# A two-layer diffusion backbone: value products of two heads side by side, modulation sums moved behind the softmax, and the feed-forward's second half reordered

## The chip, the cores and the metric

The kernel runs on one core of one Trainium2 chip. The metric is the device time of the whole program in microseconds; the smaller the better. The number of before is the median of three runs.

## What is computed

256 latent tokens and 256 context tokens, 1024 channels wide, pass through two layers in fp32. Each layer takes a modulated norm, three token mixers (a short convolution, a gated MLP along the tokens, attention with 8 heads of 64 channels and two key/value heads), a merge by gates, and a channel mixer. Layer 0 has a dense feed-forward of width 2816, layer 1 a mixture of eight experts of which each token takes two. The modulation vectors are products of one conditioning vector with a large matrix. Cut to what the change touches:

```python
m = silu(cvec) @ w_mod[i] + b_mod[i]            # shift, scale, gate, six of each layer
h = rms_norm(x, g) * (1 + scale) + shift
s = q @ k.T * HEAD_DIM ** -0.5                  # 256 latent + 256 context keys for latent tokens
p = exp(s - max) / (sum + exp(sink - max))
o = p @ v                                       # the value products
mix = sigmoid(z_gate) * (y_branch @ w_branch)   # summed over three branches, then @ w_out
y = (silu(h @ w_gate) * (h @ w_up)) @ w_down    # the feed-forward of layer 0
```

## The kernel before

The order of the work is written out by hand, and each engine takes its instructions in the order of the program. Weights come through `Stream`: a chunk is loaded from memory (L79, SyncE's queue), ScalarE rounds it to a high part (L102), and GpSimd, in layer 1 together with VectorE, subtracts to make the low part (L106). Two pairs of buffers, `w0` and `w1`, hold such chunks in layer 0. `st.take()` hands out a chunk and queues the conversion of the next one, so in ScalarE's queue the rounding of a coming chunk stands behind whatever was queued there for the chunk before. A product of fp32 accuracy is three matmuls: high by high, high by low, low by high (`prod`, L446, L447, L449).

In `mixer`, the gate products run in three passes of eight steps (`gate_pass`, argument `kb`). A step multiplies the gate weights (24 matmuls), takes tanh on ScalarE (L714), multiplies the branch weights and adds into `mix` on VectorE (L720, or L722 and L723). Between the steps `tick` runs one `slot` of the attention. Layer 0 has 16 units in the order latent head t, latent head 4+t, context head t, context head 4+t; a latent unit has four blocks of keys, a context unit two. Layer 1 has 8 latent units. Slot j does the value product of unit j-2 (`att_d`: matmuls L624 into the one PSUM buffer `pv`, a copy on ScalarE L626, a subtraction on VectorE L627), the transposes of unit j-1 (`att_c`: L603, evicted by ScalarE L607 and for four blocks also by VectorE L609), the scores of unit j (L560, L561), the query split of unit j+1 (L542, L543), and the softmax of unit j (`att_b`: row maxima on VectorE L571 or L579, exponentials on ScalarE, then L588, L589 and the scaling L591 on VectorE).

VectorE also computes the modulation vectors of later stages in the background. `bg(n)` runs n of 128 pieces; a piece is two multiply-and-sum instructions over 512 columns (L226, in `columns`), whose elementwise result goes to a scratch tile from the rotating pool `scr` (10 buffers) and is never read. The matrix rows come over SyncE's queue into the two halves of one tile `mraw` (`mod_load`, L218), each load queued one piece ahead. The pieces 0 to 95 use a load of 512 KB twice, the pieces 96 to 127 once. In layer 0's mixer a gate step runs one piece after its tanh and one after its sum, before `tick`.

The feed-forward of layer 0 runs in two halves (`hf`). Each has 11 chunks `f` of gate and up products (22 by 24 matmuls in all), whose result is split into `ah` (ScalarE, L834) and `al` (VectorE, L835), and then 8 down products `d` that add over the 11 chunks. The steps of a chunk on VectorE are: one piece, L829, L830, one piece, L835, one piece. Then layer 1's norm, its mixer, and the experts follow.

The first down product of a half starts with the chunks in order and needs `ah[10]`, made last, in its 21st matmul:

```python
for k in ks:                       # prod, ks = range(11)
    mm(p, wh(k), ah(k)); mm(p, wh(k), al(k))
for k in ks:
    mm(p, wl(k), ah(k))
```

Of the kernel before, what the change touches and what calls it, by code (L numbers as in the profile page):

```python
# [20 lines left out]
NT = 512  # L21
# [115 lines left out]
def backbone_kernel(ctx, tc, xT, small, const, moe_const, gmw, gmb, modk, modd, wa, wg2, wg4, wo, fgu, fd, mgu, mdn, fing, out):  # L137
# [83 lines left out]
    def columns(w, l, i, vs, bias=0.0):  # L221

        for v in vs:
            for h in range(2):
                o = (modv if h else mcol)[:, l, v, i:i + 1]
                nc.vector.tensor_tensor_reduce(scr(), w[:, h * 512:(h + 1) * 512], crows[:, v, h * 512:(h + 1) * 512],  # L226
                                               scale=1.0, scalar=mcol[:, l, v, i:i + 1] if h else bias,
                                               op0=OP.mult, op1=OP.add, accum_out=o)
# [52 lines left out]
    crows = crow_stack.enter_context(tc.tile_pool(name="crows", bufs=1, side="right")).tile([128, 2, D], F32, name="crows")  # L281

    def scr(dt=F32):
        return front.tile([128, 512], dt, name="scr", bufs=10)

# [178 lines left out]
    def mixer(l, kv, extra=()):  # L464
# [20 lines left out]
        def tick(cnt=1):  # L485
            for _ in range(cnt):
                if fill:
                    fill.pop(0)()

        def block(c, col, width, nn, acts=None):  # L490
# [42 lines left out]
        units = [(s, hd) for t in range(4) for s in range(ns) for hd in (t, 4 + t)]  # L533
        U = {}

        def att_q(j):
# [74 lines left out]

        def att_d(j):
            s, hd = units[j]
            t, kv = hd % 4, hd // 4
            u = U.pop(j)
            a = slice(kv * 64, kv * 64 + 64)
            nk = 4 if s == 0 else 2
            k0 = 0 if s == 0 else 2
            if t not in yh:
                yh[t] = mp.tile([128, n], F32R, name="q", bufs=5)  # L620
                yl[t] = mp.tile([128, n], F32R, name="yl", bufs=4)
            po = psum("pv")
            for kk in range(nk):
                mm(po[a, :NX], vt[:, k0 + kk, kv * 64:kv * 64 + 64], u["pT"][kk // 2][:, (kk % 2) * NX:(kk % 2 + 1) * NX],  # L624
                   start=kk == 0, stop=kk == nk - 1)
            nc.scalar.copy(yh[t][a, s * NX:(s + 1) * NX], po[a, :NX])  # L626
            nc.vector.tensor_tensor(yl[t][a, s * NX:(s + 1) * NX], po[a, :NX], yh[t][a, s * NX:(s + 1) * NX].bitcast(F32), op=OP.subtract)  # L627

        def slot(j):
            if 0 <= j - 2:  # L630
                att_d(j - 2)
            if 0 <= j - 1 < len(units):
                if extra:
                    extra.pop(0)()
                att_c(j - 1)
            if j < len(units):
                att_a(j)
                if j + 1 < len(units):
                    att_q(j + 1)
                att_b(j)  # L640
# [5 lines left out]
        for g in range(ns):  # L646
# [8 lines left out]
            if g == 0:  # L655
                rope(q[3], q[3])
                att_q(0)
                fill += [lambda j=j: slot(j) for j in range(len(units) + 2)]
            vv = gelu2(pg, NT)
# [45 lines left out]
        def gate_pass(kb, ah, al, first, ticks):  # L705
            for d in range(KD):
# [4 lines left out]
                fh, fl = H_(n)  # L711
                prod(pg, lambda k: hg[:, k, :], lambda k: lg[:, k, :], fh, fl, range(KD), n)
                tg = scr()
                nc.scalar.activation(tg[:, :n], pg[:, :n], AF.Tanh, scale=0.5)  # L714
# [6 lines left out]
                else:  # L721
                    nc.vector.scalar_tensor_tensor(tg[:, :n], tg[:, :n], 1.0, pb[:, :n], op0=OP.add, op1=OP.mult)  # L722
                    nc.vector.tensor_tensor(mix[:, d, :], mix[:, d, :], tg[:, :n], op=OP.add)  # L723
                    if kb == 4 and d == KD - 2:
                        split_mix(0)
                        split_mix(1)
                if d < KD - 2 or kb < 4:
                    bg(rate)
                tick(ticks)

# [28 lines left out]
        while fill:  # L759
            tick()  # L760
        gate_pass(4, lambda k: yh[k][:, :], lambda k: yl[k][:, :], False, 0)

# [48 lines left out]
    for hf in range(2):  # L811
        ah, al = {}, {}
        for f in range(11):
# [9 lines left out]
            else:  # L823
                for i, p in enumerate((pg, pu)):
                    prod(p, lambda k: h[:, k, i * 128:i * 128 + 128], lambda k: g[:, k, i * 128:i * 128 + 128], fh, fl, range(KD), NT)
            bg(1)
            t = scr()
            nc.scalar.activation(t, pg, AF.Tanh, scale=0.5)
            nc.vector.scalar_tensor_tensor(t, t, 1.0, pg, op0=OP.add, op1=OP.mult)  # L829
            nc.vector.tensor_tensor(t, t, pu, op=OP.mult)  # L830
            bg(1)
            ah[f] = fp.tile([128, NT], F32R, name="ah", bufs=12)
            al[f] = fp.tile([128, NT], F32R, name="al", bufs=12)
            nc.scalar.copy(ah[f], t)  # L834
            nc.vector.tensor_tensor(al[f], t, ah[f].bitcast(F32), op=OP.subtract)  # L835
            bg(1)
        if hf == 0:
# [3 lines left out]
        for d in range(8):  # L841
            c = st.take()
            h, g = (a[:, :1408].rearrange("p (k c) -> p k c", k=11) for a in (c.hi, c.lo))
            p = psum("mm")
            prod(p, lambda k: h[:, k, :], lambda k: g[:, k, :], lambda k: ah[k][:, :], lambda k: al[k][:, :], range(11), NT)
            for s in range(2):
                xs = x[:, d, s * NX:(s + 1) * NX]
                nc.vector.scalar_tensor_tensor(xs, p[:, s * NX:(s + 1) * NX], mcolumn(0, s, 5, d), xs, op0=OP.mult, op1=OP.add)
            if hf == 1:
                square(d, NT)  # L850
            if hf == 0 or d < 5:
                bg(1)
    ffn_stack.close()
# [693 lines left out]
```

## Time and profile before

| | us |
|---|---|
| median of three runs | 2093.8 (2092.99 to 2103.32) |
| the profiled execution, whole | 2096.31 |
| its span | 2094.2 |
| TensorE busy | 1922.0, 92% of the span |
| VectorE busy | 1300.0, 62% |
| ScalarE busy | 695.6 |
| GpSimd busy | 445.9 |

Times in rows count from the start of the span. Layer 0's mixer with attention lies between about 131 and 345 us, the feed-forward's second half between 632 and 837 us, layer 1's mixer between 850 and 1067 us, and the experts from there to the end. A row of a timeline gives the start, the duration (both in us), the engine, the line, the operation, the tiles written and read, the shape and a count; in brackets stands how long the engine sat idle before it and what ended that. `PE` is TensorE, `DVE` VectorE, `ACT` ScalarE, `POOL` GpSimd, `SPq` SyncE's DMA queue. [...]

### The profile page before, as it was taken

The page shows a single profiled execution, that of the slowest core. Times are in us where ns is not written, and L with a number is a line of the kernel's source. Part 1 is how long each engine was busy: PE and PEld are TensorE (multiplying, and loading weights), DVE is VectorE, ACT ScalarE, POOL GpSimd, SP SyncE. Part 2 cuts the span into 40 slices and gives each one's busy share as a digit, 9 for nine tenths or more (in the row PEclk, how much of TensorE's full clock was granted, in tenths as well). Part 3 has the DMA queues.
Part 4 walks back from the last instruction along what each step waited for, and adds up shares of the span by engine and source line. Part 5 has one row for each costly group of instructions (what it writes and reads, how often), then busy time and mean ns, then how long its engine had stood idle before and what let it go on. Part 6 is the DMA issues. An engine that isn't in the chain of part 4 may idle for free. (4 is left out here: it accounts for less than half of the span.)

```text
span 2094.2 us, 31796 instructions
## 1 busy us (share of the span) xinstructions
PE 1922.0 (92%) x9396; PEld 1304.7 (62%) x9396; DVE 1300.0 (62%) x1946; ACT 695.6 (33%) x903; POOL 445.9 (21%) x188
## 2 busy tenths in 40 slices
PE   7999889989999889899989999998999998898676
PEld 4777668878888668788987765644444444332122
DVE  7488789759967772766568866654454545442222
ACT  4334332332212212554546654433232322210000
POOL 4432234233443325524420000000000000000000
PEclk9999999999999989899999999999999999999888
DMA  6323134424444553433638989999899998899995
GB/s 265 117 67 122 51 126 161 156 90 171 154 148 173 178 192 130 154 104 106 232 123 284 323 304 365 343 376 416 323 370 354 360 365 337 332 389 408 403 387 206
DMA packets 79401, 506.04 MB, mean 242 GB/s; under 512 B 8784, under 2 KB 9424, under 8 KB 28880
## 3 DMA queue, kind: packets, MB, share of 16 engines
q1 hardware_dynamic: 79056, 501.64, 64.1%
q8 instruction: 193, 3.16, 0.6%
q14 instruction: 152, 1.25, 0.2%
HBM read 500.55 MB, written 1.05 MB: 240 GB/s over the span
## 5 line engine op out<-in xcount | busy, mean ns | idle before, releaser
L106 POOL TENSOR_TENSOR w0l<-raw,w0h 128x2048 fp32r<-128x2048 f32 (+6 forms) x43 | 156.0, 3628 | 242.2 <-ACT w0h L102 222.6
L106 POOL TENSOR_TENSOR w1l<-raw,w1h 128x2048 fp32r<-128x2048 f32 (+6 forms) x42 | 153.2, 3649 | 229.4 <-ACT w1h L102 215.5
L1221 PE MATMUL PO<-raw,Xo 128*64 128x512 f32 x768 | 186.3, 620 | 11.3 <-issue 10.0
L226 DVE CUSTOM_DVE_ANT_0 scr<-mraw,crows 128x512 f32<-128x512 f32 x128 | 165.3, 1292 | 40.7 <-DMA mraw<-in_modd_dram 40.6
L1061 POOL TENSOR_SCALAR P<-P,gates 128x256 f32<-128x256 f32 x16 | 22.1, 1392 | 758.4 <-PE PO L1048 622.0
L226 DVE CUSTOM_DVE_ANT_0 scr<-mraw,crows,mcol 128x512 f32<-128x512 f32 x128 | 161.1, 1259 | 4.6
L102 ACT CAST w1h<-raw 128x2048 fp32r<-128x2048 f32 (+3 forms) x82 | 142.2, 1735 | 43.4 <-PE mm L447 22.6
L102 ACT CAST w0h<-raw 128x2048 fp32r<-128x2048 f32 (+3 forms) x82 | 141.2, 1721 | 41.9 <-PE mm L447 28.8
L446 PE MATMUL mm<-Hh,w0h 128*128 128x512 f32 (+1 forms) x380 | 139.1, 376 | 10.7 <-ACT Hh L384 4.2
L446 PE MATMUL mm<-Hh,w1h 128*128 128x512 f32 (+1 forms) x384 | 137.1, 368 | 8.9 <-ACT w1h L102 7.1
L447 PE MATMUL mm<-Hl,w0h 128*128 128x512 f32 (+1 forms) x380 | 137.7, 372 | 6.2 <-POOL Hl L440 6.2
L447 PE MATMUL mm<-Hl,w1h 128*128 128x512 f32 (+1 forms) x384 | 135.6, 364 | 0.0
L1221 PEld LDWEIGHTS PO<-raw,Xo 128*64 128x64 f32 x768 | 55.3, 142 | 115.7 <-issue 114.3
L106 DVE TENSOR_TENSOR w1l<-raw,w1h 128x2048 fp32r<-128x2048 f32 (+3 forms) x49 | 103.5, 2112 | 30.9 <-ACT w1h L102 30.3
L1294 PE MATMUL PYO<-raw,ho 128*64 128x512 f32 x392 | 95.5, 620 | 11.4 <-issue 5.6
L106 DVE TENSOR_TENSOR w0l<-raw,w0h 128x2048 fp32r<-128x2048 f32 (+3 forms) x48 | 97.8, 2037 | 9.7 <-ACT w0h L102 9.0
L106 DVE TENSOR_TENSOR w2l<-raw,w2h 128x2048 fp32r<-128x2048 f32 (+3 forms) x45 | 90.9, 2020 | 19.5 <-ACT w2h L102 12.8
L1236 DVE SCALAR_TENSOR_TENSOR to<-to,PO 64x512 f32<-64x512 f32 x28 | 18.9, 676 | 126.0 <-ACTq L98 78.8
L1270 ACT COPY ho<-PO 128x256 f32<-128x256 f32 x42 | 15.7, 373 | 245.0 <-PE PO L1262 198.8
L449 PE MATMUL mm<-Hh,w0l 128*128 128x512 f32 (+1 forms) x380 | 94.3, 370 | 1.9 <-POOL w0l L106 1.9
L102 ACT CAST w2h<-raw 128x2048 fp32r<-128x2048 f32 (+2 forms) x45 | 81.5, 1811 | 35.6 <-PE PU L1214 26.0
L446 PEld LDWEIGHTS mm<-Hh,w0h 128*128 128x128 f32 x380 | 73.1, 192 | 25.2 <-ACT Hh L384 4.8
(469 smaller groups left out, 4253.9 us busy)
## 6 DMA issues: line engine op xcount, KB each, us to landing
raw<-in_mgu_dram SPq DMA_DIRECT2D x191, 1024.0 KB, 7.9
raw<-in_mdn_dram SPq DMA_DIRECT2D x97, 1024.0 KB, 8.5
mraw<-in_modd_dram SPq DMA_DIRECT2D x80, 512.0 KB, 4.8
mraw<-in_mgu_dram SPq DMA_DIRECT2D x33, 1024.0 KB, 8.1
raw<-in_fgu_dram SPq DMA_DIRECT2D x22, 1024.0 KB, 4.9
raw<-in_wg_dram SPq DMA_DIRECT2D x28, 640.0 KB, 3.9
raw<-in_wa_dram SPq DMA_DIRECT2D x15, 1024.0 KB, 5.0
mraw<-in_mdn_dram SPq DMA_DIRECT2D x15, 1024.0 KB, 7.4
```

The lines of the kernel that those rows point to most:

```text
L102: self.nc.scalar.copy(c.hi[:, :n], c.raw[:, :n])
L106: eng.tensor_tensor(c.lo[:, a:b], c.raw[:, a:b], c.hi[:, a:b].bitcast(F32), op=OP.subtract)
L226: nc.vector.tensor_tensor_reduce(scr(), w[:, h * 512:(h + 1) * 512], crows[:, v, h * 512:(h + 1) * 512], scale=1.0, scalar=mcol[:, l, v, i ...
L446: mm(p[:, :n], wh(k), ah(k), start=first and k == ks[0], stop=False)
L447: mm(p[:, :n], wh(k), al(k), start=False, stop=False)
L449: mm(p[:, :n], wl(k), ah(k), start=False, stop=last and k == ks[-1])
L1061: nc.gpsimd.tensor_scalar(P[:, i, :], P[:, i, :], gates[:, i, e:e + 1], None, op0=OP.mult)
L1221: mm(po[64 * g:64 * g + 64], xo[:, kk, :], w[:, k, g, :], start=kk == 0, stop=kk == KD - 1)
L1236: nc.vector.scalar_tensor_tensor(t, t, 1.0, g, op0=OP.add, op1=OP.mult)
L1270: modes(e, split, lambda: nc.scalar.copy(ho, po[:, 0:256]))
L1294: mm(PYO[64 * b:64 * b + 64], ho[:, ff, :], w[:, f, b, :], start=first and ff == 0, stop=last and ff == 3)
```

## The change

The elementwise result of a modulation piece goes into one fixed tile `junk`, and `scr` gets 14 buffers. The value products of two units, head t and head 4+t of the same tokens, become one step `att_d(m)`: their matmuls alternate between the columns 0 to 63 and 64 to 127 of the array, and one copy and one subtraction over 128 partitions take the place of two each over 64. The step isn't part of a slot any more; it is queued in `ready` once both units are transposed, and runs in `between()`, which a gate step calls behind its gate product and `tick` calls first. In a gate step, the second modulation piece comes behind `tick`. In the feed-forward's second half the last two chunks run no pieces; two more pieces run in the first half's down products, and every down product of the second half runs one. Every down product takes the chunks 0 to 9 first, with their low parts, and chunk 10 at the end. The memory set aside for DMA descriptors is cut to 2048 bytes, which makes room for the larger `scr`.

```diff
 def columns(...):
-                nc.vector.tensor_tensor_reduce(scr(), w[:, ...], crows[:, ...],
+                nc.vector.tensor_tensor_reduce(junk, w[:, ...], crows[:, ...],
...
+    junk = front.tile([128, 512], F32, name="junk")
-        return front.tile([128, 512], dt, name="scr", bufs=10)
+        return front.tile([128, 512], dt, name="scr", bufs=14)
...
         def tick(cnt=1):
             for _ in range(cnt):
+                between()
                 if fill:
                     fill.pop(0)()
+        def between():
+            while ready:
+                att_d(ready.pop(0))
...
-        def att_d(j):
+        def att_d(m):
...
+            pT = [U.pop(2 * m + kv)["pT"] for kv in range(2)]
             for kk in range(nk):
-                mm(po[a, :NX], vt[:, k0 + kk, kv * 64:kv * 64 + 64], u["pT"][...], start=kk == 0, stop=kk == nk - 1)
-            nc.scalar.copy(yh[t][a, s * NX:(s + 1) * NX], po[a, :NX])
-            nc.vector.tensor_tensor(yl[t][a, ...], po[a, :NX], yh[t][a, ...].bitcast(F32), op=OP.subtract)
+                for kv in range(2):
+                    a = slice(kv * 64, kv * 64 + 64)
+                    mm(po[a, :NX], vt[:, k0 + kk, a], pT[kv][...], start=kk == 0, stop=kk == nk - 1)
+            nc.scalar.copy(h, po[:, :NX])
+            nc.vector.tensor_tensor(l, po[:, :NX], h.bitcast(F32), op=OP.subtract)
         def slot(j):
-            if 0 <= j - 2:
-                att_d(j - 2)
             if 0 <= j - 1 < len(units):
                 ...
                 att_c(j - 1)
+                if j % 2 == 0:
+                    ready.append(j // 2 - 1)
...
 def gate_pass(...):
                 prod(pg, ...)
+                between()
                 tg = scr()
                 nc.scalar.activation(tg[:, :n], pg[:, :n], AF.Tanh, scale=0.5)
...
+                tick(ticks)
                 if d < KD - 2 or kb < 4:
                     bg(rate)
-                tick(ticks)
...
 for f in range(11):
-            bg(1)
+            rate = 1 if hf == 0 or f < 9 else 0
+            bg(rate)        # and so at the chunk's other two places
...
 for d in range(8):
-            prod(p, ..., range(11), NT)
+            for ks in (range(10), range(10, 11)):
+                prod(p, ..., ks, NT, first=ks[0] == 0, last=ks[0] > 0)
...
-            if hf == 0 or d < 5:
-                bg(1)
+            bg(2 if hf == 0 and d < 2 else 1)
...
-    nc = bacc.Bacc("TRN2", target_bir_lowering=False, num_devices=1)
+    nc = bacc.Bacc("TRN2", target_bir_lowering=False, num_devices=1, dynamic_dma_scratch_size=2048)
```

## Rows read from the trace of the kernel before

**Rows 1.** Busy time per stretch (columns: stretch, length, busy time and instruction count per engine).
```profile
133.00:231.00 98.00, 87.48 (x390) 66.25 (x388) 81.37 (x167) 37.16 (x84) 30.19 (x8) 0.97 0.30 107
260.00:314.00 54.00, 48.32 (x223) 36.57 (x222) 46.49 (x93) 19.70 (x43) 16.86 (x6) 1.00 0.35 123
750.00:800.00 50.00, 41.12 (x154) 32.41 (x153) 29.96 (x57) 10.97 (x12) 19.19 (x6) 0.86 0.51 175
```
**Rows 2.** Waits of TensorE and VectorE, layer 0's mixer (waited for: us, times, longest).
```profile
PE tp L603 <- DVE scr L591: 13.3, 10, 2.7
PE pv L624 <- DVE yl L627: 1.7, 1, 1.7
DVE tiny L588 <- ACT tiny L587: 25.0, 16, 1.8
```
**Rows 3.** Timeline of one gate step with its slot, layer 0, VectorE and GpSimd.
```profile
172.96 3.24 POOL L106 TENSOR_TENSOR w1l<-raw,w1h 128x1280 fp32r<-128x1280 f32 x1 [7.21 <-ACT w1h L102]
173.42 3.33 DVE L226 CUSTOM_DVE_ANT_0 scr<-mraw,crows,mcol 128x512 f32<-128x512 f32 x1
177.28 0.68 DVE L226 CUSTOM_DVE_ANT_0 scr<-mraw,crows 128x512 f32<-128x512 f32 x1
178.68 0.41 DVE L627 TENSOR_TENSOR yl<-pv,q 64x256 fp32r<-64x256 f32 x1
179.57 0.69 DVE L571 CUSTOM_DVE_ANT_0 scr<-sc,cst 128x512 f32<-128x512 f32 x1
183.31 0.88 DVE L591 TENSOR_SCALAR scr<-scr,tiny 128x512 f32<-128x512 f32 x2
184.11 3.45 POOL L106 TENSOR_TENSOR w0l<-raw,w0h 128x1280 fp32r<-128x1280 f32 x1 [7.91 <-ACT w0h L102]
```
**Rows 4.** Timeline of TensorE, eight matmuls of one column half and of alternating halves.
```profile
925.18 1.94 PE L624 MATMUL pv<-scr,vt 128*64 128x256 f32 x8
1299.96 1.94 PE L1221 MATMUL PO<-raw,Xo 128*64 128x512 f32 x8
```
**Rows 5.** Timeline, layer 0: last transposes kept waiting, VectorE's wait for TensorE between.
```profile
230.98 1.44 PE L603 MATMUL tp<-idn,scr 128*128 128x128 f32 x8 [2.74 <-DVE scr L591]
249.27 0.69 DVE L754 TENSOR_TENSOR cc<-cc,mm 128x512 f32<-128x512 f32 x1 [0.81 <-PE mm L449]
303.81 0.72 PE L603 MATMUL tp<-idn,scr 128*128 128x128 f32 x4 [1.63 <-DVE scr L591]
```
**Rows 6.** Timeline, layer 1: scalings of two units and the transposes that follow each.
```profile
917.86 0.88 DVE L591 TENSOR_SCALAR scr<-scr,tiny 128x512 f32<-128x512 f32 x2
919.86 1.04 PE L603 MATMUL tp<-idn,scr 128*128 128x128 f32 x8
...
968.28 0.88 DVE L591 TENSOR_SCALAR scr<-scr,tiny 128x512 f32<-128x512 f32 x2
968.92 1.29 PE L603 MATMUL tp<-idn,scr 128*128 128x128 f32 x8 [1.16 <-DVE scr L591]
```
**Rows 7.** Timeline of the feed-forward's second half, its last chunks and first down products.
```profile
752.36 0.62 ACT L834 CAST ah<-scr 128x512 fp32r<-128x512 f32 x1 [12.90 <-DVE scr L830]
754.83 0.80 PE L446 MATMUL mm<-Hh,w1h 128*128 128x512 f32 x1 [3.51 <-ACT w1h L102]
760.67 0.69 DVE L226 CUSTOM_DVE_ANT_0 scr<-mraw,crows 128x512 f32<-128x512 f32 x1
767.86 1.50 DVE L226 CUSTOM_DVE_ANT_0 scr<-mraw,crows 128x512 f32<-128x512 f32 x1 [4.30 <-DMA mraw<-in_modd_dram]
768.80 0.39 PE L446 MATMUL mm<-ah,w0h 128*128 128x512 f32 x1
778.19 0.79 PE L446 MATMUL mm<-ah,w0h 128*128 128x512 f32 x1 [4.67 <-ACT ah L834]
784.96 0.40 PE L446 MATMUL mm<-ah,w1h 128*128 128x512 f32 x1
```
**Rows 8.** Timeline, after the feed-forward: VectorE's first step of the norm's inverse root.
```profile
841.77 0.16 DVE L358 TENSOR_SCALAR tiny<-pv 128x4 f32<-128x4 f32 x1 [1.30 <-PE pv L354]
```

More of the change, by code (lines that the diff above doesn't have):

```diff
@@ L225, in columns @@
                 o = (modv if h else mcol)[:, l, v, i:i + 1]
-                nc.vector.tensor_tensor_reduce(scr(), w[:, h * 512:(h + 1) * 512], crows[:, v, h * 512:(h + 1) * 512],
+                nc.vector.tensor_tensor_reduce(junk, w[:, h * 512:(h + 1) * 512], crows[:, v, h * 512:(h + 1) * 512],
                                                scale=1.0, scalar=mcol[:, l, v, i:i + 1] if h else bias,
@@ L534, in mixer @@
         U = {}
+        ready = []
         def att_q(j):
@@ L610, in att_c @@
                 u["pT"].append(pT)
-        def att_d(j):
[L613 to L616, printed above, removed]
+        def att_d(m):
+            s, hd = units[2 * m]
+            t = hd % 4
             nk = 4 if s == 0 else 2
@@ L622, in att_d @@
             po = psum("pv")
+            pT = [U.pop(2 * m + kv)["pT"] for kv in range(2)]
             for kk in range(nk):
-                mm(po[a, :NX], vt[:, k0 + kk, kv * 64:kv * 64 + 64], u["pT"][kk // 2][:, (kk % 2) * NX:(kk % 2 + 1) * NX],
-                   start=kk == 0, stop=kk == nk - 1)
-            nc.scalar.copy(yh[t][a, s * NX:(s + 1) * NX], po[a, :NX])
-            nc.vector.tensor_tensor(yl[t][a, s * NX:(s + 1) * NX], po[a, :NX], yh[t][a, s * NX:(s + 1) * NX].bitcast(F32), op=OP.subtract)
+                for kv in range(2):
+                    a = slice(kv * 64, kv * 64 + 64)
+                    mm(po[a, :NX], vt[:, k0 + kk, a], pT[kv][kk // 2][:, (kk % 2) * NX:(kk % 2 + 1) * NX], start=kk == 0, stop=kk == nk - 1)
+            h, l = (y[t][:, s * NX:(s + 1) * NX] for y in (yh, yl))
+            nc.scalar.copy(h, po[:, :NX])
+            nc.vector.tensor_tensor(l, po[:, :NX], h.bitcast(F32), op=OP.subtract)
         def slot(j):
-            if 0 <= j - 2:
-                att_d(j - 2)
             if 0 <= j - 1 < len(units):
@@ L657, in mixer @@
                 att_q(0)
-                fill += [lambda j=j: slot(j) for j in range(len(units) + 2)]
+                fill += [lambda j=j: slot(j) for j in range(len(units) + 1)]
             vv = gelu2(pg, NT)
@@ L760, in mixer @@
             tick()
+        between()
         gate_pass(4, lambda k: yh[k][:, :], lambda k: yl[k][:, :], False, 0)
@@ L830, in backbone_kernel @@
             nc.vector.tensor_tensor(t, t, pu, op=OP.mult)
-            bg(1)
+            bg(rate)
             ah[f] = fp.tile([128, NT], F32R, name="ah", bufs=12)
@@ L835, in backbone_kernel @@
             nc.vector.tensor_tensor(al[f], t, ah[f].bitcast(F32), op=OP.subtract)
-            bg(1)
+            bg(rate)
         if hf == 0:
@@ L844, in backbone_kernel @@
             p = psum("mm")
-            prod(p, lambda k: h[:, k, :], lambda k: g[:, k, :], lambda k: ah[k][:, :], lambda k: al[k][:, :], range(11), NT)
+            for ks in (range(10), range(10, 11)):
+                prod(p, lambda k: h[:, k, :], lambda k: g[:, k, :], lambda k: ah[k][:, :], lambda k: al[k][:, :], ks, NT,
+                     first=ks[0] == 0, last=ks[0] > 0)
             for s in range(2):
```

1 line of the change is left out of this document (removed).

## The prediction

> **What bounds the kernel now.** I began with busy time by stretch. TensorE is near full everywhere, but in two stretches of layer 0's mixer it is busy for 87.5 of 98 us and 48.3 of 54 [rows 1], so 16.2 us are lost there. Then the waits: the transposes stand 13.3 us for the scaling that ends the softmax, once a value product for a subtraction, 1.7 us [rows 2]. So VectorE's queue is what is late. It is busy for 81.4 of the 98 us [rows 1]; add its wait for the exponentials, 25.0 us in 16 units [rows 2], nine of which (14 us) fall in this stretch, and it has under 3 us to spare. In layer 0's attention VectorE sets the pace, and what TensorE saves there isn't saved by the program. The timeline of a step shows on what it spends itself: a modulation piece takes 1.40 us (177.28 to 178.68), but one of its two instructions takes 3.33 when GpSimd's subtraction runs beside it, 2.6 more than usual; the row maxima, fed from PSUM, take 0.69 [rows 3]. Between the two stretches VectorE waits for TensorE (0.81 at 249.27 [rows 5]), so there TensorE sets the pace. In layer 1 no pieces run; TensorE waits for the scaling at the last unit only [rows 6]. In the feed-forward's second half the chain is: VectorE waits for a load of `mraw` (4.30 at 767.86), the product of the chunk stands behind that piece, `ah` behind the product, and in ScalarE's queue the rounding of a coming weight chunk behind `ah`: `ah` of chunk 8 at 752.36, chunk 10 on TensorE at 754.83 after 3.51 idle [rows 7]. The first down product stops 4.67 us for `ah` of chunk 10 [rows 7], and the granted clock over that stretch is 0.86 [rows 1].
>
> **The change, part by part.** All sums are made against the profiled execution, 2096.3 us, which is 2.5 above the median 2093.8.
>
> *Pairs in column halves.* Eight matmuls of one half with 256 columns take 1.94 us; eight of the experts, alternating between halves with 512 columns, take 1.94 too [rows 4]. So alternating doubles the columns per time, and a pair of latent units (16 matmuls) should take 2.0 instead of 3.9; a context pair 1.1 instead of 2.1. TensorE's work falls by 4 x 1.9 + 4 x 1.0 = 11.6 us in layer 0 and 4 x 1.9 = 7.6 in layer 1. Bounds: no overlap (0) and all of it.
>
> *Layer 0, to the wait at 230.98* [rows 5]. VectorE sets the pace, so I count VectorE's instructions. Seven subtractions of 0.41 [rows 3] become three over twice the partitions, which I price the same, since they have the same 256 columns: 4 x 0.42 = 1.7 saved. Moving the second piece behind the softmax doesn't shorten the queue: each scaling comes one piece earlier, but so does the one before it. The collision stays too: GpSimd started 0.8 us after the scaling began, which is where VectorE comes to the next piece [rows 3]; after the change it is the second piece of the same step instead of the first of the next. Taking the product buffer from `scr` to `junk` removes waits of ScalarE alone, which isn't late: nothing. From 231 to 260 TensorE sets the pace, and one interval between transposes loses a latent product: at most 1.9, less what VectorE allows; I take 1.3 (bounds 0 and 1.9). From 260 on VectorE sets the pace again. The first scaling there comes a piece earlier, 1.4 once, and one subtraction fewer, 0.4. The last wait for the subtraction, 1.7 [rows 2], goes, since the last pair follows a gate product. Sum: 1.7 + 1.3 + 1.4 + 0.4 + 1.7 = **6.5** (bounds: 0, and 27.8, if VectorE no longer bound: 16.2 + 11.6).
>
> The new position adds a wait. The pair's subtraction stands in VectorE's queue ahead of the next step's first piece, the sum into `mix` and the next softmax, and TensorE reaches the products only after 24 matmuls (24 x 0.235 = 5.6 us, from rows 4), 2.0 for the pair and some 0.6 for the copy: 8.2 us behind the scores. VectorE comes there after its softmax (179.57 to 184.2, 4.6 [rows 3]) and a piece of 1.4, or 4.0 beside GpSimd: 6.0 to 8.6 us after the scores if it begins at once. It begins late, for it is behind TensorE. I take 0; it costs up to 2.2 us per pair.
>
> *Layer 1.* A waiting transpose starts 0.64 after the scaling starts (968.28 to 968.92 [rows 6]). Of eight intervals between transposes four now hold a pair (2.0 for 1.9: nothing) and four hold none. These shorten by what TensorE was behind the scaling, at most 1.9: at the first, 2.00 - 0.64 = 1.4; at the last, nothing [rows 6]; the two between give 1.6 and 0.6 by the same difference. With one subtraction less in the last, 0.4: **4.0** (bounds: 0 and 7.6).
>
> *The feed-forward's second half.* Up to chunk 8 three pieces run per chunk as before, each with its own load of 512 KB from piece 96 on. Because two more pieces run early, this begins two pieces sooner. The waits sit at the same places of each chunk, since a load is queued when the piece two before is done; I charge 0.8 us (bounds: none, and two waits of 4.3 [rows 7], 8.6). In chunks 9 and 10 VectorE is free: its last piece of chunk 8 ends at 760.67 [rows 7], so `ah` of chunk 10 is made about 2 us after its products end at 768.80, and the first down product, which began there [rows 7], needs it only after 30 matmuls, 7 us. It then takes 33 x 0.23 = 7.6 and the second begins at 776.4 instead of 784.96 [rows 7]: 8.6. The stop at 754.83 stays. The eight pieces in the down products have 7.6 us each and lie beside matmuls; if a load is late there, the sum into `x` is late, and the cover is the three PSUM buffers. Only the last one is bare: its 1.4 us come before the norm's steps, where VectorE has 1.30 idle [rows 8]; I charge 0.4 (bounds 0 and 4.0, beside GpSimd). SyncE's queue: four more loads pass ahead of layer 1's first weights, and the weight load that reuses `mraw` waits for the last piece's 1.4 us; that is within the bound of the last piece. Sum: 8.6 - 0.8 - 0.4 = **7.4** (bounds: -4 and 12, the latter with the stop at 754.83 gone).
>
> The two extra pieces in the first half lie under a TensorE that never waits there: nothing. Together 6.5 + 4.0 + 7.4 = 17.9: 2078.4 against the profiled run, **2076** as a median.
>
> **The rivals.**
> *The collision goes.* If GpSimd's subtraction falls beside instructions fed from PSUM, the 13 gate steps with a slot lose 2.6 us each of VectorE (34 us), TensorE sets the pace in layer 0 and gains 27.8 instead of 6.5: 2055. For it: only the piece is stretched, the row maxima aren't [rows 3]. Against: GpSimd follows the exponentials by one rounding, and the piece follows them by the scaling, before and after. [...] Half of it would still be 2066.
> *The load waits give the feed-forward back.* Two more single loads at 4.3 us delay `ah` of chunk 8 by 8.6: that part gives 0, total 10.5: 2083.
> *The halves don't overlap.* Pairs cost 3.9: layer 1 loses 1.9 in three of four intervals and layer 0 where TensorE sets the pace (3.7): 17.9 - 9.4 = 8.5: 2085. Rows 4 speak against it.
> *TensorE's clock eats layer 0's part.* TensorE now idles longer at each scaling; at 750 to 800 us, with 9 us idle of 50, 0.86 was granted [rows 1]. If the 152 us of layer 0's two stretches ran so, TensorE would need some 20 us more, about what it has to spare: 6.5 becomes 0, 2082.
> *Slower: VectorE stands at the pair's subtraction.* If TensorE, not VectorE, is late, every one of the 12 pairs stops VectorE, with the next softmax behind it. It takes back all at 1.5 us per pair (17.9/12) and costs over 0.5% at 2.4. If the eight of layer 0 wait a whole gate product, 8 x 5.6 = 45: 2121. Against: VectorE has no idle time there but for the exponentials.
>
> **How the numbers follow.** Forecast 0.57, spread about 2067 to 2084; collision gone 0.07; load waits 0.12; no overlap 0.07; clock 0.09; slower 0.08. The range 2062 to 2089 leaves out the slower case, most of the first rival and the tails of the others, just under 2 in 10. About 0.5%, 10.5 us, is what a measurement of this kernel can tell from no change; so faster is below 2083.3. Faster: 0.52 + 0.07 + 0.05 + 0.01 + 0.06 = 0.71. Within: 0.05 + 0.07 + 0.06 + 0.03 = 0.21. Slower: 0.08.
>
> **What would show it.** Right: value products as 12 groups of 16 or 8 matmuls with about 0.12 us each; L627 twelve times at 0.42; layer 0's transposes still waiting for L591, more in sum than 13.3 us; a piece of 3.3 us in each gate step; in the feed-forward stops near chunks 7, 8 and 10, and none at the first down product; 0.4 us before the norm. Wrong: VectorE idle at L627, no stretched pieces in layer 0, or a stop at a down product.

## The result and the profile after

The changed kernel takes 2079.06 us (median; 2075.30 to 2093.04) against 2093.39 before (2088.21 to 2103.32). The ratio is 0.9938, with a 95% interval of 0.9918 to 0.9958: faster by 14.3 us, or by 9 to 17. The forecast was 2076. The profiled execution took 2076.99 us with a span of 2075.2; that of before took 2096.31 with 2094.2. Of these two, one lies 2.1 below its median and the other 2.9 above, so the traces show 19 us where the medians show 14.

The way to read two traces of one program is to set the starts of the same events side by side. The starts below are TensorE's; the last column is what the span has gained up to there, beside the forecast's sum at that point.

| event | before | after | gained | forecast |
|---|---|---|---|---|
| layer 0, 1st transposes | 140.21 | 140.66 | -0.5 | 0 |
| layer 0, 9th transposes | 230.98 | 230.14 | 0.8 | 1.7 |
| layer 0, 13th transposes | 269.38 | 265.48 | 3.9 | 4.8 |
| layer 0, last transposes | 303.81 | 298.37 | 5.4 | 4.8 |
| first norm | 440.81 | 434.84 | 6.0 | 6.5 |
| feed-forward, second half | 631.88 | 626.45 | 5.4 | 6.5 |
| its first down product | 768.80 | 762.53 | 6.3 | 5.7 |
| its second down product | 784.96 | 770.06 | 14.9 | 14.3 |
| second norm | 839.87 | 824.94 | 14.9 | 13.9 |
| layer 1, first transposes | 911.33 | 895.35 | 16.0 | 13.9 |
| layer 1, eighth transposes | 968.92 | 950.11 | 18.8 | 17.9 |
| third norm | 1067.02 | 1050.20 | 16.8 | 17.9 |
| end of the span | 2094.2 | 2075.2 | 19.0 | 17.9 |

TensorE reaches the first transposes of layer 0 without waiting in every kernel of this document, and starts them anywhere from 139.9 to 141.7 us. That spread lies ahead of what the change does, so differences in layer 0 are also counted from there below.

The page of after shows where the engines stand. TensorE is busy for 92% of the span:

```profile
PE 1903.7 (92%) x9396; PEld 1299.3 (63%) x9396; DVE 1295.3 (62%) x1934; ACT 690.9 (33%) x891; POOL 447.8 (22%) x188
```

Next is the timeline of TensorE with the value products and the transposes: start, duration, operation and, in brackets, idle time and what ended it. The first row is a pair of latent units in layer 1, the second a context pair in layer 0; then come the transposes that answer to [rows 5] and [rows 6].

```profile
907.42 1.95 PE L634 MATMUL pv<-scr,vt 128*64 128x256 f32 x16
180.35 1.08 PE L634 MATMUL pv<-scr,vt 128*64 128x256 f32 x8
...
230.14 1.29 PE L611 MATMUL tp<-idn,scr 128*128 128x128 f32 x8 [2.09 <-DVE scr L599]
298.37 0.72 PE L611 MATMUL tp<-idn,scr 128*128 128x128 f32 x4 [1.73 <-DVE scr L599]
950.11 2.06 PE L611 MATMUL tp<-idn,scr 128*128 128x128 f32 x8 [2.59 <-DVE scr L599]
```

Sixteen matmuls of a pair take 1.95 us, what eight in one half took [rows 4]. So the change does what it says. The waits of layer 0's mixer answer to [rows 2] (waited for: us, times, longest):

```profile
PE tp L611 <- DVE scr L599: 17.0, 8, 3.7
...
DVE tiny L596 <- ACT tiny L595: 25.0, 16, 1.8
```

TensorE now stands longer at the scaling, 17.0 us instead of 13.3 (its 1.7 us at the subtraction are gone), and VectorE's wait for the exponentials hasn't moved. This is what a saving looks like on an engine that wasn't the bound: its work shrinks and its waits grow. The busy times per stretch answer to [rows 1] (length; PE, PEld, DVE, ACT and POOL busy; then TensorE's granted clock as a share of full speed, DMA share and GB/s):

```profile
133.00:231.00 98.00, 85.87 (x397) 66.40 (x396) 80.82 (x166) 35.83 (x80) 30.39 (x8) 0.93 0.30 107
260.00:314.00 54.00, 49.90 (x237) 38.42 (x236) 46.62 (x88) 19.99 (x41) 20.00 (x6) 0.97 0.33 119
750.00:800.00 50.00, 48.84 (x214) 40.03 (x215) 18.59 (x34) 12.29 (x14) 29.53 (x10) 1.00 0.40 139
```

VectorE's 80.8 of 98 us are the 81.4 of before. The third stretch is the feed-forward's: 0.86 was granted there before and 1.00 now. Half of that lies behind the stop ahead of chunk 10 (0.82 from 750.0 to 768.8 before) and half in the first down product, whose stop is gone (0.79 from there to 784.96). A gate step of layer 0 answers to [rows 3]: GpSimd's subtraction and the two instructions of a piece beside it.

```profile
171.91 0.69 DVE L226 CUSTOM_DVE_ANT_0 junk<-mraw,crows 128x512 f32<-128x512 f32 x1
172.18 3.20 POOL L106 TENSOR_TENSOR w1l<-raw,w1h 128x1280 fp32r<-128x1280 f32 x1 [7.06 <-ACT w1h L102]
172.64 3.29 DVE L226 CUSTOM_DVE_ANT_0 junk<-mraw,crows,mcol 128x512 f32<-128x512 f32 x1
```

The collision has stayed. Up to layer 0's last transposes 12 piece instructions are stretched in either kernel, by 32.3 us in all before and 32.5 after (over the usual 0.72). The feed-forward's second half answers to [rows 7] and [rows 8]: the matmul of chunk 10 that had to wait, the roundings to `ah` of chunks 8 and 10, the starts of the first two down products, the last piece's instruction and the norm's first step.

```profile
749.98 0.50 PE L448 MATMUL mm<-Hh,w1h 128*128 128x512 f32 x1 [2.61 <-ACT w1h L102]
747.51 0.62 ACT L847 CAST ah<-scr 128x512 fp32r<-128x512 f32 x1 [12.89 <-DVE scr L843]
763.45 0.62 ACT L847 CAST ah<-scr 128x512 fp32r<-128x512 f32 x1 [4.04 <-DVE scr L843]
762.53 0.40 PE L448 MATMUL mm<-ah,w0h 128*128 128x512 f32 x1
770.06 0.39 PE L448 MATMUL mm<-ah,w1h 128*128 128x512 f32 x1
...
824.80 0.68 DVE L226 CUSTOM_DVE_ANT_0 junk<-mraw,crows 128x512 f32<-128x512 f32 x1
826.86 0.16 DVE L360 TENSOR_SCALAR tiny<-pv 128x4 f32<-128x4 f32 x1
```

The rounding to `ah` of chunk 10 starts 0.92 us after the first down product does, and that product takes 7.53 us without a stop; before it took 16.16 [rows 7]. The step of the norm at 826.86 no longer waits.

### The profile page after: what moved, and what is told of

Read it like the earlier page. It is cut to its first block, busy times and chain, and to the rows that moved or that the text cites. A ratio compares the mean times of both kernels' runs of the same rounds, so it can differ in the third digit from the quotient of the medians.

```text
span 2075.2 us, 31786 instructions
## 1 busy us (share of the span) xinstructions
PE 1903.7 (92%) x9396; PEld 1299.3 (63%) x9396; DVE 1295.3 (62%) x1934; ACT 690.9 (33%) x891; POOL 447.8 (22%) x188
## 5 line engine op out<-in xcount | busy, mean ns | idle before, releaser
L106 POOL TENSOR_TENSOR w1l<-raw,w1h 128x2048 fp32r<-128x2048 f32 (+6 forms) x42 | 155.2, 3695 | 227.2 <-ACT w1h L102 227.2
L106 POOL TENSOR_TENSOR w0l<-raw,w0h 128x2048 fp32r<-128x2048 f32 (+6 forms) x43 | 155.2, 3610 | 226.8 <-ACT w0h L102 222.8
L226 DVE CUSTOM_DVE_ANT_0 junk<-mraw,crows,mcol 128x512 f32<-128x512 f32 x128 | 192.0, 1500 | 4.6
L226 DVE CUSTOM_DVE_ANT_0 junk<-mraw,crows 128x512 f32<-128x512 f32 x128 | 141.9, 1109 | 36.0 <-DMA mraw<-in_modd_dram 34.9
L448 PE MATMUL mm<-Hh,w1h 128*128 128x512 f32 (+1 forms) x384 | 137.4, 369 | 10.5 <-ACT w1h L102 8.6
L1285 ACT COPY ho<-PO 128x256 f32<-128x256 f32 x42 | 15.7, 373 | 243.9 <-PE PO L1277 184.1
L448 PEld LDWEIGHTS mm<-Hh,w1h 128*128 128x128 f32 x384 | 75.3, 196 | 23.8 <-ACT w1h L102 9.9
```

Of the source, the lines that this page charges most:

```text
L106: eng.tensor_tensor(c.lo[:, a:b], c.raw[:, a:b], c.hi[:, a:b].bitcast(F32), op=OP.subtract)
L226: nc.vector.tensor_tensor_reduce(junk, w[:, h * 512:(h + 1) * 512], crows[:, v, h * 512:(h + 1) * 512], scale=1.0, scalar=mcol[:, l, v, i: ...
L448: mm(p[:, :n], wh(k), ah(k), start=first and k == ks[0], stop=False)
L1285: modes(e, split, lambda: nc.scalar.copy(ho, po[:, 0:256]))
```

## The experiments

Times without an interval are single ones. A single time of this kernel moves by several us, so I judge those kernels by starts inside the trace, up to the third norm. In layer 0 even a start differs by up to 1.8 us ahead of any edit (the spread of the first transposes), so there the distance from the first transposes decides.

### The feed-forward, taken apart

Three kernels are before with the feed-forward's edits: all of them, the new order of the down products alone, and the moved pieces alone.

```diff
 # e2_order_only
-prod(p, ..., range(11), NT)
+for ks in (range(10), range(10, 11)):
+    prod(p, ..., ks, NT, first=ks[0] == 0, last=ks[0] > 0)
 # e3_moves_only
-bg(1)                               # three places of a chunk
+bg(1 if hf == 0 or f < 9 else 0)
-if hf == 0 or d < 5:
-    bg(1)                           # down products
+bg(2 if hf == 0 and d < 2 else 1)
 # e1_ff_only: both
```

> The kernel before with the feed-forward's edits alone: no pieces in the last two chunks of the second half, the pieces spread over the down products, chunk 10 last in each down product. If the prediction's reason holds (the stop at the first down product goes), the second down product of the second half begins 8 to 10 us sooner than before (784.96 us there), with the mixers as before, and the program takes 8 to 10 us less. Rival (the moved loads give it back): the stops ahead of chunks 7 to 10 grow by about as much and the time stays within 2 us of before.

> The kernel before with the order of the down products alone changed (chunk 10 last). If the late piece in VectorE's queue is the cause, ah of chunk 10 is still made near 777.5 us while TensorE now needs it 7 to 9.6 us after 768.8, so most of the stop of 4.7 goes and the second down product begins 2 to 7 us sooner. If the order does the work and the pieces don't matter, it begins all 8.6 us sooner.

> The kernel before with the pieces moved out of the last two chunks, but the old order of the down products. If the pieces are the cause, ah of chunk 10 comes about 2 us after its products end, ahead of the 21st matmul (4.6 us in), so the stop goes without the new order and the second down product begins 8 to 9.5 us sooner. If the order is what counts, a stop of over 2 us stays at the first down product.

The feed-forward's part alone gave 2082.29 us, a ratio of 0.9954 (0.9929 to 0.9979). Order alone took 2085.80, moves alone 2080.82. From the start of the second half to its second down product, and to the second norm, the traces show:

| kernel | to the second down product | to the second norm |
|---|---|---|
| before | 153.1 | 208.0 |
| order alone | 148.2 | 205.2 |
| moves alone | 143.4 | 198.3 |
| both, without the mixers' part | 143.3 | 198.2 |
| after | 143.6 | 198.5 |

With the order alone TensorE still waits for `ah` of chunk 10, only later and for a shorter time (compare the 4.67 us of [rows 7]):

```profile
777.26 0.63 PE L446 MATMUL mm<-ah,w0h 128*128 128x512 f32 x1 [2.07 <-ACT ah L834]
```

With the moves alone there is no stop in the first down product:

```profile
768.37 0.40 PE L446 MATMUL mm<-ah,w0h 128*128 128x512 f32 x1
775.90 0.39 PE L446 MATMUL mm<-ah,w1h 128*128 128x512 f32 x1
```

So the moved pieces do it all. The order is worth 4.9 us at the second down product by itself, and nothing beside them: once VectorE's queue is free of pieces in the last two chunks, `ah` of chunk 10 is in time for either order.

### One half after the other

```diff
 # e4_one_half (from after)
-for kk in range(nk):
-    for kv in range(2):
+for kv in range(2):
+    for kk in range(nk):
```

> The changed kernel, but the matmuls of a pair run first in one column half, then in the other, all else alike. If alternating halves run side by side, a latent pair takes 3.8 to 3.9 us here instead of 1.95; layer 1 up to the last transposes is 4 to 6 us longer, layer 0's mixer 1 to 4 us longer (there VectorE sets the pace and hides the rest). If the halves overlap anyhow, or the gain comes from the merged copies alone, both stay within 1 us.

I expected that all matmuls of one half, then all of the other, wouldn't overlap. They do in part:

```profile
924.66 2.86 PE L634 MATMUL pv<-scr,vt 128*64 128x256 f32 x16
178.48 1.09 PE L634 MATMUL pv<-scr,vt 128*64 128x256 f32 x8
```

A context pair (four and four) takes 1.09 us, no more than alternating, and a latent pair (eight and eight) 2.86, between the 1.95 of after and twice the 1.94 of [rows 4]. So this kernel was no clean test of the overlap. What 0.9 us more per latent pair cost is still readable: in layer 1, from the first to the eighth transposes, 56.5 us instead of 54.8, that is 1.7 for the pairs in between. The time was 2088.11.

### The two heads apart

To take the overlap away for certain, I put other matmuls between the two heads of a pair: the last eight of the gate product.

```diff
 # e12_apart (from after; att_d now takes the head of the pair as part)
-prod(pg, hg, lg, fh, fl, range(KD), n)
-between()
+...            # the 16 matmuls of the high parts
+between(0)     # value product of the pair's first head
+...            # the 8 matmuls with the low parts
+between(1)     # the second head, copy and subtraction
```

> The changed kernel with the two heads of a pair set apart: one ahead of the last eight matmuls of the gate product, the other behind them, copies as in the changed kernel. Nothing can run side by side now, and a latent pair should take 2 x 1.9 us. If the overlap carries layer 1's gain, layer 1 from its norm to the next one is 3 to 6 us longer than the 225.3 of the changed kernel, layer 0's mixer up to the norm 1 to 4 us longer. If the merged copies carry it, both stay within 1 us.

Each head now takes what it took before:

```profile
924.57 1.94 PE L641 MATMUL pv<-scr,vt 128*64 128x256 f32 x8
927.58 1.94 PE L641 MATMUL pv<-scr,vt 128*64 128x256 f32 x8
```

From the first to the eighth transposes of layer 1 this kernel takes 58.8 us, before 57.6 and after 54.8. The overlap is worth 4.0 in the new order of work, and this order without the overlap would have been 1.2 slower than before: all of layer 1's gain is the overlap. In layer 0 the first norm comes at 436.34, only 1.5 later than in after (0.9 from the first transposes), though the same 11.6 us of TensorE's work are back. The time was 2084.42.

### The piece ahead of the softmax again

```diff
 # e5_piece_first (from after)
-tick(ticks)
 if d < KD - 2 or kb < 4:
     bg(rate)
+tick(ticks)
```

> The changed kernel with the second modulation piece of a gate step back ahead of the softmax. By the prediction the move is worth 1.4 us once in layer 0, where VectorE sets the pace: the last transposes there (298.4 us in the changed kernel) and the norm after the mixer (434.8) come 1 to 3 us later, nothing changes behind. If the move is what makes the mixer faster, they come 5 us or more later, back at the times of before (303.8 and 440.8).

The wait of TensorE for the scaling in layer 0's mixer rises from 17.0 to 21.8 us:

```profile
PE tp L611 <- DVE scr L599: 21.8, 9, 4.9
```

The last transposes come at 300.69 (2.3 later than in after) and the first norm at 435.87 (1.0 later); the time was 2077.77. From the first transposes it is 2.6 and 1.4. The 2.6 come in two places: 1.2 up to the ninth transposes and 1.4 from the thirteenth to the last. A piece's place in the queue is worth about one piece in each stretch where VectorE sets the pace, not one per step. VectorE now also waits in layer 0 at the pair's subtraction:

```profile
DVE yl L637 <- ACT q L636: 1.9, 3, 1.0
```

### Layer 0 without the pieces

These two kernels, from before and from after, leave out the modulation pieces in the gate steps of layer 0: a constant is written in place of their sums. The loads stay.

```diff
 # e6_light_before, e7_light_after
-nc.vector.tensor_tensor_reduce(...)     # both halves of the piece, in gate steps
+nc.vector.memset(modv[:, l, v, i:i + 1], 0.01)
```

> The kernel before, leaving out the two long instructions of each modulation piece that runs in layer 0's gate steps (a constant is written instead; the loads stay). If VectorE sets the pace there, TensorE's stops of 16.2 us between 131 and 345 us shrink to under 5 and the norm after the mixer comes 12 to 20 us sooner than 440.8. If TensorE sets the pace, it comes under 5 us sooner.

> The changed kernel with the same pieces left out. If VectorE hid TensorE's saving of 11.6 us on the value products, it shows here: the norm after layer 0's mixer comes 8 to 12 us sooner than with the same left out of the kernel before, and the collision's rival time (27.8 us sooner than before in all) is about reached. If the saving wasn't hidden, the difference is the 6 us that the two full kernels show.

Without pieces the old kernel reaches the first norm at 422.54, 18.3 us sooner. TensorE's wait for the scaling falls to a single one, and VectorE now waits for TensorE:

```profile
PE tp L614 <- DVE scr L602: 2.4, 1, 2.4
DVE scr L733 <- PE mm L460: 48.4, 12, 6.8
...
133.00:231.00 98.00, 95.57 (x442) 73.21 (x442) 51.61 (x142) 43.49 (x95) 29.59 (x9) 0.98 0.30 107
```

TensorE is busy for 95.6 of the same 98 us. So it is VectorE's queue that set the pace, as read from [rows 1] and [rows 2]. With the new mixer the first norm comes at 412.42, which is 10.1 sooner than without it. The new mixer saves 10.1 us where TensorE sets the pace and 6.0 in the kernel as it is. The two together gain 28.4 (440.81 to 412.42), against the 27.8 that the prediction put down as the bound of layer 0's part.

### The buffer of the piece's result

```diff
 # e8_scr_out (from after)
-nc.vector.tensor_tensor_reduce(junk, w[:, ...], crows[:, ...],
+nc.vector.tensor_tensor_reduce(scr(), w[:, ...], crows[:, ...],
```

> The changed kernel with the unread result of each modulation instruction written to the rotating scratch pool again (14 buffers, 4 of them per gate step), in place of the one fixed tile. By the prediction the fixed tile is worth nothing: the norm after layer 0's mixer stays within 1 us of 434.8 and the second norm within 2 us of 824.9. Rival (the pool's turn-over makes VectorE or ScalarE wait): 2 us or more later.

The first norm came at 433.53, 1.3 sooner than in after (0.6 from the first transposes), and the third at 1049.48, 0.7 sooner. The fixed tile is worth nothing. No run tests the larger pool, 14 buffers instead of 10, by itself. The time was 2084.12; what puts it above after lies behind the third norm, where the two kernels are the same.

### What the reasons point to

If VectorE's queue sets layer 0's pace, the 25.0 us in which it waits for the exponentials are the place for a piece. And if the feed-forward's second half loses its time to pieces that wait for a load each, three per chunk are too many: two, with the rest moved to the first half's down products, should stop nothing.

```diff
 # e10_piece_in_wait (from after), in the softmax
 nc.scalar.activation(es[:, :2], nm[:, :2], AF.Exp, bias=sk)
+bg(rate)
 # ... and in the gate step, its first piece
-if d < KD - 2 or kb < 4:
+if kb == 4 and d < KD - 2:
     bg(rate)
 # e9_two_per_chunk (from after), in a chunk
-bg(rate)
+bg(1 if hf == 0 else 0)     # first place
-bg(rate)
+bg(1)                       # second and third place
 # ... and in the down products
-bg(2 if hf == 0 and d < 2 else 1)
+bg(2 if hf == 0 else 1)
 # e11_both: both
```

> The changed kernel with the first modulation piece of each gate step with a slot moved into the softmax, where VectorE waits 1.6 us for the exponentials (25.0 us in 16 units). If VectorE sets the pace in layer 0, this gives back 1.4 us per unit less what it delays the scaling: the norm after layer 0's mixer comes 6 to 15 us sooner than 434.8 and TensorE's stops fall below 10 us. Rival: the later scaling, or a new collision with GpSimd, takes the gain, and it stays within 3 us.

> The changed kernel with the modulation pieces spread more evenly in the feed-forward: two in each down product of the first half, two (not three) in each chunk of the second half, one in each of its down products but the last. If three loads per chunk against one chunk's time on TensorE cause the stops that are left (ahead of chunks 6, 8 and 10, 11.0 us with those for the low parts, and the low clock behind them), they go, and the distance from the first norm to the second falls from 390.1 to 374 to 378 us. If the collision with GpSimd causes them, stops of several us stay.

> Both of these edits on the changed kernel. They lie in different stages, so the gains should add: 18 to 30 us less than the changed kernel, 2049 to 2061 us. If one stage's gain is given back in the next, the sum falls short by over 5 us.

| kernel | us | ratio to before, 95% | first norm | second norm | third norm |
|---|---|---|---|---|---|
| after | 2079.06 | 0.9938 (0.9918 to 0.9958) | 434.84 | 824.94 | 1050.20 |
| piece in the wait | 2062.58 | 0.9867 (0.9848 to 0.9886) | 417.25 | 807.79 | 1033.43 |
| two per chunk | 2065.71 | 0.9875 (0.9849 to 0.9901) | 434.80 | 808.81 | 1035.14 |
| both | 2046.93 | 0.9791 (0.9769 to 0.9813) | 416.92 | 790.40 | 1015.86 |

The piece in the wait gave 17.6 us at the first norm, more than I had expected. The waits of layer 0's mixer with it:

```profile
PE tp L612 <- DVE scr L600: 7.8, 4, 4.6
DVE tiny L597 <- ACT tiny L595: 3.1, 8, 0.4
...
174.58 0.75 DVE L226 CUSTOM_DVE_ANT_0 junk<-mraw,crows,mcol 128x512 f32<-128x512 f32 x1
175.72 0.16 DVE L597 TENSOR_TENSOR tiny<-tiny 128x2 f32<-128x2 f32 x1 [0.38 <-ACT tiny L595]
177.64 3.32 DVE L226 CUSTOM_DVE_ANT_0 junk<-mraw,crows,mcol 128x512 f32<-128x512 f32 x1
```

VectorE's wait falls from 25.0 us to 3.1 and TensorE's from 17.0 to 7.8. The piece in the wait runs at its usual 0.75; the other one of the step still collides. Up to the last transposes nine instructions are stretched instead of twelve, 23.3 us instead of 32.5, which I had not counted on. The run doesn't separate these 9.2 us from what filling the wait gave. With two pieces per chunk TensorE doesn't stop in the feed-forward's second half (each chunk takes 11.0 us, and VectorE is busy for 58 of 80 us):

```profile
680.00:760.00 80.00, 80.00 (x351) 65.71 (x350) 58.03 (x82) 21.43 (x22) 33.08 (x8) 1.00 0.55 183
```

The rival in this run's expectation, that the collision with GpSimd makes the stops, is refuted by the same trace. From the start of the half to its first down product 11 piece instructions are still stretched, by 39.0 us in all, where after has 10 and 40.9. What fell is VectorE's wait for the loads, over the same chunks in after and then here:

```profile
DVE junk L226 <- DMA mraw<-in_modd_dram: 25.4, 12, 3.6
```
```profile
DVE junk L226 <- DMA mraw<-in_modd_dram: 13.5, 11, 2.5
```

The two gains add: the version with both is faster than after by 32 us, and than before by 46.

## Why the prediction was right, and where its steps were not

**What sets the pace.** Right, and shown: taking pieces out of VectorE's queue gains 18.3 us in the old kernel, where TensorE's work isn't touched; taking 11.6 us out of TensorE, with all else in the new mixer, gains 6.0.

**Layer 0, 6.0 for 6.5.** The sum held better than its terms, and in part by luck. Four subtractions were to bring 1.7 to the ninth transposes; counted from the first, 1.3 came. But with the piece ahead of the softmax again only 0.1 of it is left (90.7 us from the first to the ninth; 90.8 before, 89.5 after), as VectorE then waits at the pair's subtraction. So the piece's place counts in this stretch, where the prediction put it at nothing. Between the ninth and the thirteenth 3.1 came for 3.1, and half of that is luck. In the profiled execution of before the granted clock was low behind the wait at 230.98; the kernel with the feed-forward's part alone has the same mixer and kept the full clock. The two, over 12 us from the ninth transposes:

```profile
230.98:242.98 12.00, 12.00 (x52) 9.07 (x53) 9.05 (x21) 4.82 (x11) 2.76 (x1) 0.86 0.00 0
```
```profile
232.30:244.30 12.00, 12.00 (x61) 9.24 (x62) 9.14 (x21) 5.51 (x12) 2.77 (x1) 1.00 0.00 0
```

Before takes 38.4 us from the ninth to the thirteenth, that kernel and the one with the order alone 36.9, after 35.3. So the new mixer brought about 1.5 there, and the low clock, which this mixer shows in some executions and not in others, the rest. From the thirteenth to the last transposes 1.5 came where nothing was put down. It is the piece's place (34.3 with it undone, 34.4 before, 32.9 after), whose 1.4 the prediction had one stretch earlier. Behind the last transposes 0.5 came for 1.7. From the first transposes to the norm the part is worth 6.4 against before, and 4.9 against the same mixer at the full clock. That the place is not worth a piece per step was right, and that `junk` gives nothing too.

**The collision.** It was said to stay, and it stayed: 12 stretched instructions, 32.3 us and 32.5. The trace shows what it costs either side: at 172.18 GpSimd starts while the piece's first instruction still runs (0.69 us from 171.91, its usual time), and takes 3.20 us, where it mostly takes 2.95 in the kernels without pieces; the piece's second instruction, 0.46 us later, takes 3.29. It ends 0.55 us behind GpSimd's (175.93 and 175.38), as before (176.75 and 176.20 [rows 3]). With a piece put into the wait, the second instruction of the step's other piece is still stretched (3.32). For the rival in which the collision goes, the row maxima of [rows 3] show nothing, as they lie at 179.57, between two subtractions of GpSimd. In after, two instructions that read PSUM and lie beside one keep a short time, 0.42 us at 207.11 and 0.68 at 218.93 (GpSimd takes 5.04 from 206.61 and 5.01 from 218.41), while the next on VectorE, which reads no PSUM, takes 4.76 and 4.05. What failed of that rival is its condition: the piece stayed where GpSimd's subtraction is.

**The halves overlap.** The rival that they don't is refuted by the rows of 1.95 and 1.08 us, and the kernel with the heads apart shows what they are worth: 4.0 us of layer 1.

**The new wait at the pair's subtraction.** It was taken as 0, with up to 2.2 us per pair as the bound and as the slower case. All the subtractions of after, with VectorE's idle time before them (count, then durations; idle us, times):

```profile
L637 DVE TENSOR_TENSOR yl<-pv,q x12: 411/416/425, 165.6 to 957.9; 128x256 fp32r<-128x256 f32 x12
...
  ACT q L636: 0.4, 1
```

Twelve of 0.416 us, as priced, and one wait of 0.4. The slower rival isn't there, for the reason given: VectorE comes late to everything but the exponentials. The margin is thin, though. With the piece ahead of the softmax the wait is there in layer 0 (1.9 us, three times), and in the new kernel without pieces, where TensorE is the late one, seven of layer 0's eight pairs stop VectorE, for 19.8 us.

**Layer 1: the sum right, one term by chance.** 3.9 us to the eighth transposes, for 4.0. But 1.1 of them come ahead of the first transposes, where nothing was forecast: of the matmuls from 880.31 on, most of the first eleven came every 0.12 us where they had come every 0.21 before, though the stop ahead of them was as long (1.86 us). That has nothing to do with the pairs: from the second norm to the first transposes the kernels take 70.4 to 71.5 us with either mixer. Between the first and the eighth the pairs brought 2.8, for 4.0. And 2.0 were given back behind them, the step that failed. After the longer stop, 2.59 us instead of the 1.16 of [rows 6], the transposes took 2.06 us instead of 1.29, and the granted clock of the next 25 us was lower. After and before, over the same work:

```profile
950.00:975.00 25.00, 24.89 (x198) 23.81 (x199) 14.12 (x31) 9.26 (x13) 11.10 (x6) 0.93 0.35 114
```
```profile
968.80:993.80 25.00, 24.88 (x204) 23.72 (x204) 15.13 (x32) 9.62 (x14) 12.67 (x6) 1.00 0.39 132
```

0.07 of 25 us is 1.75, nearly all of the 2.0. The prediction had the clock as a rival, but in layer 0, and counted on nothing of it here. All kernels together show both halves of this, since layer 1's code differs only by the mixer (the two that change how a pair is multiplied are left out):

| stretch of layer 1 | 5 kernels, old mixer | 7 kernels, new mixer |
|---|---|---|
| first to eighth transposes | 57.6 | 54.6 to 55.3 |
| eighth transposes to third norm | 98.1 to 98.8 | 98.1 and 98.6 in two, 99.9 to 100.4 in five |
| first transposes to third norm | 155.7 to 156.3 | 152.8 to 155.2 |

The stop ahead of the eighth transposes is 2.5 to 2.6 us long in all seven, so its length alone doesn't decide. In the two that lost nothing, one with the piece ahead of the softmax and one without pieces, the clock stayed at 1.00 behind a stop of the same 2.59 us. The first of them:

```profile
950.30:975.30 25.00, 24.99 (x212) 23.85 (x213) 14.71 (x31) 9.19 (x14) 12.78 (x6) 1.00 0.41 134
```

Why it fell in five and not in these two stays open. So layer 1's part is worth about 3 us until the last units, and at the norm about 1 where the clock fell and 3 where it held, not 4.

**The clock in layer 0.** The granted clock fell there from 0.97 to 0.93 and from 1.00 to 0.97, so the rival of the clock was half present. In the first stretch it cost nothing, as VectorE sets the pace. The kernel with two pieces per chunk has the same mixer, and in its trace the first stretch had 0.97:

```profile
PE tp L611 <- DVE scr L599: 19.4, 9, 3.6
...
133.00:231.00 98.00, 83.49 (x397) 64.25 (x395) 80.93 (x167) 35.75 (x81) 30.48 (x8) 0.97 0.30 107
```

With the faster clock TensorE waits 19.4 us for the scaling instead of 17.0, and from the first transposes to the ninth the two take 89.6 and 89.5 us, to the first norm 294.3 and 294.2.

**The feed-forward, 9.5 for 7.4.** The core was right: 8.6 between the two down products' starts were forecast, and 8.6 is what the traces give (16.16 to 7.53). The charges were not. For the loads 0.8 was deducted, and 0.8 was gained (136.9 us from the start of the half to the first down product, 136.1 after). The stops up to there did not shrink: they sum to 11.0 us where they were 10.3, and the first sits one chunk earlier (chunks 6, 8 and 10 instead of 7, 8 and 10). What changed for the better is the granted clock, 1.00 in the last 18.8 us ahead of the first down product, where it was 0.82. The three stops for a high part, 9.6 us before:

```profile
PE mm L448 <- ACT w1h L102: 8.6, 3, 3.6
```

The rival that saw two more load waits delay `ah` of chunk 8 by 8.6 us is refuted: its rounding starts 121.1 us into the half, before 120.5. With the first down product's 5.4 gone, all of TensorE's stops in the half fell from 15.7 to 11.0 us. For the last piece 0.4 was charged; nothing was lost: from the second down product to the norm either kernel takes 54.9, and VectorE's first step of the norm starts 1.9 us behind that in both. The stops cost more here than their length: without any stop the way to the second down product takes 128.4 us (two per chunk), so before lost 24.7 with 15.7 of stops and after 15.2 with 11.0. What the stops don't explain are slow matmuls behind them, such as the 0.80 of [rows 7] and the 0.50 at 749.98, where 0.39 is usual. The forecast held this for the down product, since it took its 16.2 us from the trace, and not for the loads.

**The sum.** Up to the third norm 16.8 us for 17.9; the feed-forward's surplus makes up for layer 1's loss, and the slow clock in before's trace for what layer 0 lacks. 2.2 more came behind it, in the experts, whose code is the same; no run separates them from the spread of single executions (with the piece's result in `scr` the same stretch took 7.8 us more than in after). By medians the change is worth 14.3, and the forecast lies 3 us too fast, at the edge of the interval. The one part that was isolated with an interval, the feed-forward, is worth 9.6 us by its ratio (4 to 15). So some 5 remain for the mixers, no more certain than that, where 10.5 were forecast and the traces show 6.0 and 1.9.

## What to carry to other kernels

Find the engine whose queue sets the pace of a stretch, and count a change in that queue: 11.6 us off TensorE, with what else the new mixer does, gave 5 to 6 here, since TensorE's waits grew in the place of its work. An engine that waits in order for a round trip through another one is the place for background work: one piece put into VectorE's wait for the exponentials gave 17.6 us, without a single instruction less, though up to 9.2 of them may be collisions that went with it. And when background work feeds on loads, its rate has to fit them: two pieces per chunk instead of three gave 16 us, more than all the rearranging at the end of that half.

## What the runs showed of the hardware

Two halves of the array's columns overlap without alternating as well, to a degree: four matmuls of 256 columns in one half took 1.08 us (before), four in one and then four in the other 1.09, alternating 1.08; eight and eight took 2.86, alternating 1.95, and with other matmuls between the two halves 1.94 each. I had expected 3.8 for eight and eight. And a longer stop of TensorE went with a lower granted clock behind it: 1.4 us more of stop at layer 1's last unit with 0.93 instead of 1.00 over 25 us, 1.75 us as an estimate from these two. It did so in five of seven kernels with that stop; in two the clock stayed at 1.00.
